# Stick-breaking attention by a running product: one sigmoid a score, the mask on another engine, the halves of the output added at the branch

## The chip, the core and the metric

The kernel runs on one core of one Trainium2 chip. The metric is the device time of one execution in microseconds (us). A measurement is the median of several executions; the profiles shown are one execution each. The core has five engines with an instruction queue each: PE (TensorE, matrix products), DVE (VectorE), ACT (ScalarE), POOL (GpSimd) and SP (SyncE, which here only issues DMAs). POOL issues DMAs too. An engine works through its queue in order: an instruction that waits holds up all that stand behind it.

## The reference

One decoder block on 1024 tokens of width 1024, all in float32. Three attention branches work on the normed input: stick-breaking attention (8 heads of 64), forgetting attention (8 heads of 64, called fox in the kernel) and attention over 256 memory tokens (4 heads of 128). Each branch has an output projection and a gate; the gated sum goes through `w_out`, then a squared-ReLU MLP follows. The part that the change touches:

```python
def stick_breaking_attention(q, k, v):
    # A[t,s] = beta[t,s] * prod_{s<j<t}(1-beta[t,j]), strictly causal
    ...
        z = einsum('bhtd,bhsd->bhts', q_block, k[:kend]) * scale
        strict = s_idx < t_idx
        log_rem = where(strict, log_sigmoid(-z), 0.0)
        after = cumsum(log_rem, axis=3, reverse=True) - log_rem
        w = where(strict, exp(log_sigmoid(z) + after), 0.0)
        out = einsum('bhts,bhsd->bhtd', w, v)
...
merged = gates[0] * (o_sb @ w_branch_sb) + gates[1] * (o_fox @ w_branch_fox) + gates[2] * (o_mem @ w_branch_mem)
x = x + merged @ w_out
```

With beta = sigmoid(z), what is left of the stick at token s is L[s], the product of sigmoid(-z) over the tokens from s to t; the weight of s is L[s+1] - L[s].

## The kernel before

**Split operands.** Every float32 operand of a product is kept as two tiles of 128 partitions, a rounded high part (`whi`, or the first half of an `h` tile) and the rest (`wlo`, or the second half). A product takes three matmuls: high by high, low by high, high by low. The high part is an ACT copy (L1054), the low part a DVE subtraction (L1055).

**Order of the work.** For about the first 925 us, each engine's order of instructions is set by a planner in the kernel: small programs (Python generators) yield `Op(engine, cost, ...)`, `Get(places)` for a free tile and events, and a machine model with the costs written in the kernel decides who goes next on each engine. The order is fixed before the run; at run time the engines only wait on semaphores. The output projection and the MLP behind it come in a fixed order of their own.

**Stick-breaking.** There are four pairs of heads. A unit is one head and 256 query rows (`g` of 4), that is two tiles of 128 rows; `UNITS` gives the order. `sb_tile` works through a tile's keys in chunks of up to 512 columns from the last to the first: PE makes the scores (L824) in a bank of PSUM; on the chunk with the diagonal DVE adds the mask, a tile `later` with a large number at the places not allowed (L834); ACT makes two sigmoids, `rho` = sigmoid(-z) in a scratch tile (L827, place from `RQ`) and sigmoid(z) (L828); DVE scans them backwards, state = rho * state + sigmoid(z) (L843), which is 1 - L. PE turns the result by 128x128 blocks (L917); ACT copies the turned bank as the high part `pth` (L922) and DVE makes the low part `ptl` (L924); PE multiplies with the split values (L934), whose rows were prepared as differences of neighbouring values by `value_step`.

**Output of a unit.** The product has 128 rows: the sums with the high and with the low half of the values, 64 rows each. For stick-breaking, ACT copies one half to `ob` (L962), DVE adds the other (L963), and one 64x256 store goes to `o_scr[0]` (L965). For fox, ACT copies all 128 rows (L953) and two stores put the halves in `o_scr[1]` and `low_scr` (L957, L958); `sums_kept` turns the softmax sums of a pair by PE (L614), ACT copies them (L616) and SP stores them in `l_scr` (L618).

**Branches.** `fetched_o(bi, k)` loads rows k of a branch's output as a 128x1024 tile from a place in `RR` (L1663); for fox (`bi` 2) it loads the low half too (L1666), adds it (L1668), and multiplies by the sums (L1672, L1675). `bring` then splits the tile as an operand. `dense_branch` runs the products (L1144) in the order memory, stick-breaking, fox (`bi` 0, 1, 2), multiplies by the gate (L1779, L1781, gates loaded at L1740) and adds (L1783). `RR` has three tiles of 128x1024; two of them serve as four `rho` tiles until the four stick-breaking pairs are over (`whole_again`), and `RR` then has all three again, with four `e` tiles more once all pairs are over.

**POOL** issues the loads of heads' keys and queries (L1004, L581) and of weights (L1062).

## Time and profile before

| what | value |
|---|---|
| device time, median of 3 runs | 1685.86 us (1685.47 to 1686.56) |
| profiled execution, first to last instruction | 1686.7 us |
| PE busy | 1675.3 us, 99% |
| DVE busy | 1293.0 us, 77% |
| ACT busy | 848.9 us, 50% |
| POOL busy | 255.2 us, 15% |
| DMA | 284.32 MB, mean 169 GB/s |

The profiled execution's span is 0.8 us above the median of the runs and 0.1 above their highest; no other time of that execution is shown. A line such as `L828 ACT ACTIVATE e<-pp 128x512 ... x31 | 17.3, 558 | 0.0` reads: line 828 of the kernel, engine, operation, output tile from input tile, shape, number of instructions, then busy time in us and mean of one in ns, then the engine's idle time just before them with what ended it. In a timeline a row begins with its start and its length in us; a bracket gives the idle time before it and what it waited for. A view of windows gives the busy time of each engine in a stretch, then the clock granted to PE (1.00 is full speed), the share of the DMA engines' time and the rate in GB/s.

### The profile page before, as it was taken

The page shows a single profiled execution, that of the slowest core. Times are in us where ns is not written, and L with a number is a line of the kernel's source. Part 1 is how long each engine was busy: PE and PEld are TensorE (multiplying, and loading weights), DVE is VectorE, ACT ScalarE, POOL GpSimd, SP SyncE. Part 2 cuts the span into 40 slices and gives each one's busy share as a digit, 9 for nine tenths or more (in the row PEclk, how much of TensorE's full clock was granted, in tenths as well). Part 3 has the DMA queues.
Part 4 walks back from the last instruction along what each step waited for, and adds up shares of the span by engine and source line. Part 5 has one row for each costly group of instructions (what it writes and reads, how often), then busy time and mean ns, then how long its engine had stood idle before and what let it go on. Part 6 is the DMA issues. An engine that isn't in the chain of part 4 may idle for free.

```text
span 1686.7 us, 25003 instructions
## 1 busy us (share of the span) xinstructions
PE 1675.3 (99%) x9118; PEld 1432.0 (85%) x9118; DVE 1293.0 (77%) x2079; ACT 848.9 (50%) x1474; POOL 255.2 (15%) x440
## 2 busy tenths in 40 slices
PE   9999999999999999999999999999999999999999
PEld 9998899998888888888888887878888887888887
DVE  7977778855459888867877898987777776688775
ACT  6455555534358888866761446433333344332331
POOL 0000000000253151254400011022111120000000
PEclk9999999999999999999999999999999999999999
DMA  7445434467475365387747542144444484564532
GB/s 245 157 150 182 149 119 150 146 194 243 127 232 161 111 186 151 117 240 224 236 146 245 183 162 100 57 162 155 152 150 137 150 307 171 202 202 143 198 125 75
DMA packets 142221, 284.32 MB, mean 169 GB/s; under 512 B 16913, under 2 KB 53329, under 8 KB 142098
## 3 DMA queue, kind: packets, MB, share of 16 engines
q1 hardware_dynamic: 110562, 183.08, 32.0%
q0 software_dynamic: 31536, 99.64, 19.5%
q8 instruction: 72, 1.18, 0.3%
q14 instruction: 51, 0.42, 0.1%
HBM read 189.83 MB, written 92.83 MB: 168 GB/s over the span
## 4 chain that ended last, share of the span: by engine, by line
PE 92%; DVE 5%; DMA 2%; ACT 1%; issue 1%; SPq 0%; DVEq 0%; ACTq 0%
PE pp L1456 11%; PE pp L1144 10%; PE pp L1981 10%; PE pp L2658 8%; PE sc L1456 7%; PE sc L1144 6%; PE sc L1981 5%; PE sc L2658 4%; PE tr L2658 4%; PE tr L917 4%; PE pv L1456 3%; PE pv L2658 3%; PE tr L1981 2%; PE sc L934 2%; PE pp L934 2%; DVE h L1917 1%
## 5 line engine op out<-in xcount | busy, mean ns | idle before, releaser
L1055 DVE TENSOR_TENSOR wlo<-raw,whi 128x1024 fp32r<-128x1024 f32 (+1 forms) x88 | 107.5, 1222 | 80.2 <-ACT whi L1054 80.0
L1054 ACT ACTIVATE whi<-raw 128x1024 fp32r<-128x1024 f32 (+1 forms) x88 | 93.2, 1059 | 78.8 <-PE pp L1456 32.7
L2658 PE MATMUL pp<-h,sop 128*128 128x512 f32 x540 | 128.4, 396 | 0.0
L2658 PEld LDWEIGHTS pp<-h,sop 128*128 128x128 f32 x540 | 101.6, 188 | 24.4
L1981 PE MATMUL pp<-h,oh 128*128 128x512 f32 x384 | 121.1, 397 | 0.7 <-ACT cu L2066 0.6
L924 DVE TENSOR_TENSOR ptl<-tr,pth 128x512 fp32r<-128x512 f32 (+1 forms) x160 | 99.1, 628 | 24.1 <-ACT pth L922 23.1
L922 ACT ACTIVATE pth<-tr 128x512 fp32r<-128x512 f32 (+1 forms) x160 | 87.4, 556 | 36.0 <-PE sc L934 15.8
L1981 PEld LDWEIGHTS pp<-h,oh 128*128 128x128 f32 x384 | 72.0, 188 | 19.0 <-ACT cu L2066 1.4
L2573 ACT ACTIVATE h<-t 128x2048 fp32r<-128x2048 f32 (+1 forms) x17 | 30.7, 1814 | 110.2 <-DVE t L1917 97.4
L1373 POOL DMA_DIRECT2D raw<-w_in x32 | 24.2, 755 | 395.1 <-DVE wlo L1055 395.1
L1144 PE MATMUL sc<-h,whi 128*128 128x512 f32 (+1 forms) x254 | 77.7, 389 | 0.0
L1456 PE MATMUL pp<-h,whi 128*128 128x512 f32 x248 | 77.5, 394 | 0.0
L1981 PE MATMUL pp<-h,ol 128*128 128x512 f32 x192 | 76.1, 396 | 0.0
L1456 PE MATMUL pp<-whi,h 128*128 128x256 f32 x384 | 71.8, 283 | 0.0
L843 DVE TENSOR_TENSOR_SCAN e<-r,e 128x384 f32<-128x384 f32 (+3 forms) x64 | 66.3, 1044 | 6.9 <-ACT e L828 6.5
L1974 ACT ACTIVATE oh<-raw 128x512 fp32r<-128x512 f32 x64 | 39.4, 625 | 61.8 <-DVE raw L1917 61.8
L2658 PE MATMUL sc<-h,sop 128*128 128x512 f32 x264 | 63.7, 396 | 0.0
L2658 PE MATMUL tr<-h,sop 128*128 128x512 f32 x264 | 63.4, 396 | 0.0
L1917 DVE TENSOR_TENSOR sop<-ur,sop 128x2048 fp32r<-128x2048 f32 (+1 forms) x28 | 61.8, 2211 | 2.0 <-ACT sop L2586 2.0
L917 PE MATMUL tr<-ident,e 128*128 128x128 f32 x416 | 62.7, 273 | 0.0
L1456 PEld LDWEIGHTS pp<-whi,h 128*128 128x128 f32 x384 | 60.2, 188 | 0.0
L2658 PEld LDWEIGHTS sc<-h,sop 128*128 128x128 f32 x264 | 49.6, 188 | 12.3 <-DVE sop L1917 0.5
(558 smaller groups left out, 5087.7 us busy)
## 6 DMA issues: line engine op xcount, KB each, us to landing
ur<-s_scr SPq DMA_DIRECT2D x26, 1024.0 KB
raw<-w_in POOLq DMA_DIRECT2D x42, 512.0 KB, 4.9
raw<-w_up SPq DMA_DIRECT2D x60, 256.0 KB
...
```

Of the source, the lines that this page charges most:

```text
L843: nc.vector.tensor_tensor_scan(out=back, data0=rho[:, :u][:, ::-1], data1=back, initial=0.0 if last else beta[:, c + u:c + u + 1], op0=ALU ...
L917: nc.tensor.transpose(tr[:, jj * 256 + a * P:jj * 256 + (a + 1) * P], es[a][:, j * P:(j + 1) * P], ident)
L922: yield Op("ACT", act_time(512 - lo_c), lambda: nc.scalar.activation(ph[:, lo_c:], tr[:, lo_c:], AF.Copy))
L924: yield Op("DVE", dve_time(512 - lo_c), lambda: nc.vector.tensor_tensor(pl[:, lo_c:], tr[:, lo_c:], f32(ph[:, lo_c:]), ALU.subtract))
L934: nc.tensor.matmul(pv[0][:, c_:256], pair.v[:, j, b, :], p_[:, jj * 256 + c_:(jj + 1) * 256], start=(k == 0 and n_ == 0 and i == 0), stop= ...
L1054: yield Op("ACT", 0.03 + act_time(m), lambda: nc.scalar.activation(hi, raw, AF.Copy))
L1055: yield Op("DVE", dve_time(m), lambda: nc.vector.tensor_tensor(lo, raw, f32(hi), ALU.subtract))
L1144: nc.tensor.matmul(ps, a_, b_, start=(first and i == 0), stop=(last and i == n - 1))
L1456: nc.tensor.matmul(out_, a_, b_, start=(first and n == 0 and j == 0), stop=(last and n == 3 and j == len(todo) - 1), skip_group_check=True)
L1917: nc.vector.tensor_tensor(out_, a_, b_, op)
L1981: nc.tensor.matmul(ps, w[a_][:, k * P:(k + 1) * P], h[b_][k], start=(first and k == 0 and i == 0), stop=(last and k == 3 and i == 2), skip ...
L2658: nc.tensor.matmul(ps, a_[:, c, qs], b_[:, c, :], start=(kind in ("P1", "P2", "P7") and c == 0 and i == 0), stop=(kind in ("P2", "P4", "P3 ...
```

## The change

- `sb_tile` makes one sigmoid a chunk, of the scaled score, straight into the tile `left` (L827); the other sigmoid goes, and with it the scratch tiles (`RQ`).
- The mask is no longer added to the scores by DVE. On the diagonal block, behind the sigmoid, POOL writes ones at the places that aren't allowed (an affine select of 128x128, L833).
- The scan is a product of what is left, in place, with a broadcast zero as the second operand and 1.0 at its start (L838).
- At the turned copy ACT adds minus one (a bias that is a pointer to a column of constants, L917) and DVE does the same with a number (L920), for stick-breaking only.
- The values' difference changes its sign (`value_step`).
- A stick-breaking unit's output is copied whole (L949) and stored as two halves, in `o_scr[0]` and `low_scr[0]` (L953, L954), as fox does. `fetched_o` for that branch takes two tiles of `RR`, loads both halves (L1645, L1648) and DVE adds them (L1649).
- All three tiles of `RR` are free from the start of the attention part, and `whole_again` goes.

Unchanged code stands up to eighteen lines earlier than before: turns at L911, the copies at L917 and L920, products of values at L931, sums of fox at L613 to L619, splits at L1044 and L1045, branch products at L1134, gates at L1727.

```diff
...
-    sm = C.p.tile([P, 8], F32, tag="sm", name="sm")
-    zero, one = sm[:, 0:1], sm[:, 1:2]
+    sm = C.p.tile([P, 9], F32, tag="sm", name="sm")
+    zero, one, minus = sm[:, 0:1], sm[:, 1:2], sm[:, 8:9]
...
+    nc.vector.memset(minus, -1.0)
...
-    low_scr = dram.tile([512, S], F32, name="low_scr", tag="low_scr")
+    low_scr = [dram.tile([512, S], F32, name=f"low_scr{b}", tag=f"low_scr{b}") for b in range(2)]
...
-    def sb_tile(pair, b, i, beta):
+    def sb_tile(pair, b, i, left):
...
         def chunk(ci, c, m, u):
-            rho = yield Get(RQ)
             sc = yield Get(SC)
+            part = left[:, c:c + u]
 
             def scores():
                 nc.tensor.matmul(sc[:, :m], q, pair.t["k1", b, ci][:, :m], start=True, stop=False)
                 nc.tensor.matmul(sc[:, :m], q, pair.t["k2", b, ci][:, :m], start=False, stop=True)
-
-            def sigmoids():
-                nc.scalar.activation(rho[:, :u], sc[:, :u], AF.Sigmoid, scale=HD ** -0.5)
-                nc.scalar.activation(beta[:, c:c + u], sc[:, :u], AF.Sigmoid, scale=-HD ** -0.5)
-
             yield Op("PE", 2 * mm_time(max(m, 256)), scores)
+            yield Op("ACT", act_time(u), lambda: nc.scalar.activation(
+                part, sc[:, :u], AF.Sigmoid, scale=HD ** -0.5), table=AF.Sigmoid)
+            SC.put(sc)
             last = c + u == n
             if last:
-                dg = sc[:, u - P:u]
-                yield Op("DVE", 0.22, lambda: nc.vector.tensor_tensor(
-                    dg, dg, holder["later"][:, 385:513], ALU.add))
-            yield Op("ACT", act_time(u, u), sigmoids, table=AF.Sigmoid)
-            SC.put(sc)
-            if not last:
+                dg = left[:, n - P:n]
+                yield Op("POOL", 0.3, lambda: nc.gpsimd.affine_select(
+                    out=dg, in_=dg, pattern=[[-1, P]], compare_op=ALU.is_ge, fill=1.0, base=-1, channel_multiplier=1))
+            else:
                 yield scanned
-
-            def scan():
-                back = beta[:, c:c + u][:, ::-1]
-                nc.vector.tensor_tensor_scan(out=back, data0=rho[:, :u][:, ::-1], data1=back,
-                                             initial=0.0 if last else beta[:, c + u:c + u + 1],
-                                             op0=ALU.mult, op1=ALU.add)
-            yield Op("DVE", 0.1 + 0.00215 * u, scan, 0.14)
-            RQ.put(rho)
+            back = part[:, ::-1]
+            yield Op("DVE", 0.1 + 0.00215 * u, lambda: nc.vector.tensor_tensor_scan(
+                out=back, data0=back, data1=zero.to_broadcast([P, u]),
+                initial=1.0 if last else left[:, c + u:c + u + 1], op0=ALU.mult, op1=ALU.add), 0.14)
             if last:
                 machine.fire(scanned)
 
...
-        scr, r0 = o_scr[0 if pair.kind == "sb" else 1], (2 * pair.p + b) * HD
+        of_sb = pair.kind == "sb"
+        scr, low, r0 = o_scr[0 if of_sb else 1], low_scr[0 if of_sb else 1], (2 * pair.p + b) * HD
...
             ph = yield Get(PH)
-            yield Op("ACT", act_time(512 - lo_c), lambda: nc.scalar.activation(ph[:, lo_c:], tr[:, lo_c:], AF.Copy))
+            h_, t_ = ph[:, lo_c:], tr[:, lo_c:]
+            yield Op("ACT", act_time(512 - lo_c), lambda: nc.scalar.activation(
+                h_, t_, AF.Identity, bias=minus) if of_sb else nc.scalar.activation(h_, t_, AF.Copy))
             pl = yield Get(PL)
-            yield Op("DVE", dve_time(512 - lo_c), lambda: nc.vector.tensor_tensor(
-                pl[:, lo_c:], tr[:, lo_c:], f32(ph[:, lo_c:]), ALU.subtract))
+            yield Op("DVE", dve_time(512 - lo_c), lambda: nc.vector.scalar_tensor_tensor(
+                pl[:, lo_c:], t_, -1.0, f32(h_), ALU.add, ALU.subtract) if of_sb else nc.vector.tensor_tensor(
+                pl[:, lo_c:], t_, f32(h_), ALU.subtract))
...
         ob = yield Get(OB)
         rows, cols = slice(r0, r0 + HD), slice(g * 256, (g + 1) * 256)
-        if pair.kind == "fox":
-            yield Op("ACT", act_time(256), lambda: nc.scalar.activation(ob, pv[0][:, :256], AF.Copy))
-            PV.put(pv[0])
-
-            def halves():
-                nc.sync.dma_start(scr[rows, cols], ob[:HD, :])
-                nc.sync.dma_start(low_scr[rows, cols], ob[HD:, :])
-            yield Op("SP", 0.2, halves, 3.0)
-        else:
-            o = ob[:HD, :]
-            yield Op("ACT", act_time(256), lambda: nc.scalar.activation(o, pv[0][HD:P, :256], AF.Copy))
-            yield Op("DVE", dve_time(256), lambda: nc.vector.tensor_tensor(o, o, pv[0][0:HD, :256], ALU.add))
-            PV.put(pv[0])
-            yield Op("SP", 0.1, lambda: nc.sync.dma_start(scr[rows, cols], o), 2.5)
+        yield Op("ACT", act_time(256), lambda: nc.scalar.activation(ob, pv[0][:, :256], AF.Copy))
+        PV.put(pv[0])
+
+        def halves():
+            nc.sync.dma_start(scr[rows, cols], ob[:HD, :])
+            nc.sync.dma_start(low[rows, cols], ob[HD:, :])
+        yield Op("SP", 0.2, halves, 3.0)
...
     def value_step(c, g, a, b, more):
         yield Sleep(3.0)
-        yield Op("DVE", dve_time(512), lambda: nc.vector.tensor_tensor(a, a, b, ALU.subtract))
+        yield Op("DVE", dve_time(512), lambda: nc.vector.tensor_tensor(a, b, a, ALU.subtract))
...
         opened("A", (HT, "h", 12, 512, F32R), (VV, "v", 2, 2048, F32R), (EL, "e", 4, D, F32), (RR, "r", 3, D, F32),
-               (LATER, "later", 1, 513, F32))
+               (LATER, "later", 1, 512, F32))
         later = holder["later"] = LATER.free[0]
-        halves = [RR.free.popleft() for _ in range(2)]
-        RQ.put(*(t[:, i * 512:(i + 1) * 512] for t in halves for i in range(2)))
-        spawn(whole_again(halves))
...
-    def whole_again(tiles_):
-        for pair in pairs[:4]:
-            yield pair.over
-        RR.put(*tiles_)
-
...
     def fetched_o(bi, k):
 
-        raw_ = yield Get(RR)
+        raw_, *low_ = (yield Get(RR, 2)) if bi == 1 else [(yield Get(RR))]
         raw, rows = raw_[:, :S], slice(k * P, (k + 1) * P)
         yield from transfer(lambda: nc.sync.dma_start(raw, o_scr[order[bi][1]][rows, :]), P * S * 4)
+        if bi == 1:
+            t = low_[0]
+            yield from transfer(lambda: nc.sync.dma_start(t, low_scr[0][rows, :]), P * S * 4)
+            yield Op("DVE", dve_time(S), lambda: nc.vector.tensor_tensor(raw, raw, t, ALU.add))
+            RR.put(t)
         if bi == 2:
             t = yield Get(RR)
-            yield from transfer(lambda: nc.sync.dma_start(t, low_scr[rows, :]), P * S * 4)
+            yield from transfer(lambda: nc.sync.dma_start(t, low_scr[1][rows, :]), P * S * 4)
             yield Sleep(1.0 if k == ks[3] else 2.0)
             yield Op("DVE", dve_time(S), lambda: nc.vector.tensor_tensor(raw, raw, t, ALU.add))
```

The planner orders its part anew. PE's order is the same up to about 485 us of the trace before, and from about 922 us on.

**SP where the memory branch ends and the stick-breaking branch begins.** Before (near 881 us of the trace), L1663 loads `r_4694` and `r_4696` for fox, L1666 the low half for fox; the four loads of the stick-breaking branch stand further ahead and aren't in these rows:

```order
L957 DMA o_scr_75<-ob_4803 64x256
L958 DMA low_scr<-ob_4803 64x256
L1663 DMA r_4694<-o_scr_75 128x1024
L1740 DMA o_4811<-gate_scr 128x512
L618 DMA l_scr<-ob_4805 16x128
L1740 DMA o_4810<-gate_scr 128x512
L1666 DMA r_4695<-low_scr 128x1024
L1663 DMA r_4696<-o_scr_75 128x1024
```

After, with `o_scr_75` and `low_scr_78` the halves of stick-breaking, `o_scr_76` and `low_scr_79` those of fox:

```order
L1648 DMA r_4697<-low_scr_78 128x1024
L953 DMA o_scr_76<-ob_4804 64x256
L954 DMA low_scr_79<-ob_4804 64x256
L1727 DMA o_4812<-gate_scr 128x512
L1727 DMA o_4813<-gate_scr 128x512
L619 DMA l_scr<-ob_4806 16x128
L1645 DMA r_4697<-o_scr_75 128x1024
L1645 DMA r_4696<-o_scr_76 128x1024
L1645 DMA e_4692<-o_scr_76 128x1024
L1648 DMA r_4698<-low_scr_78 128x1024
L1653 DMA e_4693<-low_scr_79 128x1024
L1653 DMA e_4694<-low_scr_79 128x1024
```

The last operand of the stick-breaking branch is now loaded in two halves behind the store of the fox sums, with two fox loads between them and two behind.

**PE at the same place.** Before (`whi_163`, `wlo_164` and `h_7212` are split outputs of stick-breaking, `whi_167` and `wlo_168` weights):

```order
L1144 MATMUL sc_136<-whi_163,whi_167 128x512
L1144 MATMUL sc_136<-wlo_164,whi_167 128x512
L1144 MATMUL sc_136<-whi_163,wlo_168 128x512
L1144 MATMUL sc_136<-h_7212,whi_167 128x512 x2
L1144 MATMUL sc_136<-h_7212,wlo_168 128x512
L1144 MATMUL pp_134<-whi_163,whi_167 128x512
L1144 MATMUL pp_134<-wlo_164,whi_167 128x512
L1144 MATMUL pp_134<-whi_163,wlo_168 128x512
L614 MATMUL tr_139<-ident,fn 16x128
```

After (`whi_165`, `wlo_166` and `h_7517` are split outputs of stick-breaking, the other `h` tiles earlier ones, `whi_169` and `wlo_170` weights):

```order
L1134 MATMUL pp_136<-h_4681,whi_169 128x512
L1134 MATMUL pp_136<-h_4687,whi_169 128x512
L1134 MATMUL pp_136<-h_4681,wlo_170 128x512
L615 MATMUL tr_140<-ident,fn 16x128
L1134 MATMUL sc_138<-whi_165,whi_169 128x512
L1134 MATMUL sc_138<-wlo_166,whi_169 128x512
L1134 MATMUL sc_138<-whi_165,wlo_170 128x512
L1134 MATMUL sc_138<-h_7517,whi_169 128x512 x2
L1134 MATMUL sc_138<-h_7517,wlo_170 128x512
```

The turn of the fox sums, which stood behind the first products of the last two stick-breaking operands, now stands three products ahead of the first that needs `h_7517`.

**DVE at the same place, after.** `r_4696` and `r_4697` are stick-breaking outputs that are summed at L1649:

```order
L1649 TENSOR_TENSOR r_4696<-r_4696,r_4697 128x1024
L613 RECIPROCAL fn<-fn 128x16
L1045 TENSOR_TENSOR h_7518<-r_4698,h_7518 128x512
L1045 TENSOR_TENSOR wlo_166<-r_4696,whi_165 128x512
L1045 TENSOR_TENSOR h_7518<-r_4698,h_7518 128x512
L1045 TENSOR_TENSOR wlo_166<-r_4696,whi_165 128x512
L1045 TENSOR_TENSOR wlo_168<-raw_171,whi_167 128x1024
L1649 TENSOR_TENSOR r_4697<-r_4697,r_4698 128x1024
L1045 TENSOR_TENSOR h_7517<-r_4697,h_7517 128x512 x2
```

The reciprocal that the turn of the fox sums needs stands behind the first sum, and the split of `h_7517` behind the second; before there were no sums here.

**SP at the memory branch's loads.** Before (near 727 us):

```order
L965 DMA o_scr_74<-ob_4805 64x256
L703 DMA o_scr_76<-o_4811 128x512
L1641 DMA gate_scr<-o_4810 128x512
L1663 DMA r_4696<-o_scr_76 128x1024
L1663 DMA r_4694<-o_scr_76 128x1024
L1663 DMA r_4695<-o_scr_76 128x1024
```

After, where the memory attention ends later in the order:

```order
L704 DMA o_scr_77<-o_4812 128x512
L619 DMA l_scr<-ob_4806 16x128
L1645 DMA r_4698<-o_scr_77 128x1024
L1645 DMA r_4696<-o_scr_77 128x1024
L1645 DMA r_4697<-o_scr_77 128x1024
```

The three loads now stand behind a store of fox sums.

**POOL in the stick-breaking part, after.** Selects stand between loads of heads' keys and queries; before, this queue had loads only:

```order
L833 AFFINE_SELECT es_4809<-es_4809 128x128
L833 AFFINE_SELECT es_4810<-es_4810 128x128
L582 DMA h_4820<-mq_scr_92 128x512
L582 DMA h_4818<-mq_scr_93 128x512
L994 DMA h_4685<-sbk_scr_86 64x512 x2
L994 DMA h_4814<-sbk_scr_87 64x512 x2
L994 DMA h_4683<-sbk_scr_86 64x512 x2
L994 DMA h_4817<-sbk_scr_87 64x512 x2
L994 DMA h_4819<-sbq_scr_84 64x512
L994 DMA h_4819<-sbq_scr_85 64x512
```

The next select (`es_4807`) follows these loads.

4 lines of the change are left out of this document (2 added, 2 removed).

## The prediction

> **What bounds the kernel now.** I read the page's busy times, then the waits of PE, then windows and timelines of the planned part. The first is a line of the page, the second the two longest waits of PE (engine, line waited for: total, times, longest), the third two stretches of 100 us.
>
> ```profile
> PE 1675.3 (99%) x9118; PEld 1432.0 (85%) x9118; DVE 1293.0 (77%) x2079; ACT 848.9 (50%) x1474; POOL 255.2 (15%) x440
> ```
> ```profile
> PE pp L2305 <- ACT h L2280: 1.5, 1, 1.5
> PE pv L869 <- DVE st L874: 1.5, 1, 1.5
> ```
> ```profile
> 600.00:700.00 100.00, 100.00 (x625) 88.19 (x624) 87.82 (x162) 89.39 (x197) 32.88 (x60) 1.00 0.55 163
> 700.00:800.00 100.00, 98.53 (x609) 86.03 (x608) 73.77 (x202) 70.21 (x158) 45.66 (x85) 0.98 0.72 213
> ```
>
> PE is the bound: 1675.3 of 1686.7 us, and in the stick-breaking stretch (600 to 700) it is full although ACT and DVE also stand near 88%. An instruction taken from ACT or DVE there gives nothing by itself. Only one stall lies in the part that the change touches: 1.5 us at L869, at 742.59. The timelines of SP, ACT and PE, and windows around it (PE, PEld, DVE, ACT, POOL busy, granted clock, DMA share, GB/s):
>
> ```profile
> 731.58 0.33 SPq L1663 DMA_DIRECT2D r<-o_scr  x1
> ```
> ```profile
> 740.50 0.63 ACT L1054 ACTIVATE h<-r 128x512 fp32r<-128x512 f32 x1 [3.58 <-DMA r<-o_scr]
> ```
> ```profile
> 742.59 0.50 PE L869 MATMUL pv<-h,h 128*128 128x512 f32 x1 [1.47 <-DVE st L874]
> ```
> ```profile
> 742.00:744.00 2.00, 1.41 (x6) 1.05 (x7) 2.00 (x7) 1.72 (x4) 0.00 (x0) 0.94 0.98 340
> 744.00:746.00 2.00, 2.00 (x6) 1.52 (x6) 0.81 (x5) 1.91 (x4) 0.00 (x0) 0.50 0.98 320
> 746.00:748.00 2.00, 2.00 (x13) 1.70 (x12) 0.70 (x2) 0.46 (x2) 0.00 (x0) 0.71 0.81 308
> ```
>
> A 512 KB load issued at 731.58 landed at 740.5, 8.9 us later, with the DMA near full; ACT stood behind it for 3.58 us, and what PE waited for stood behind ACT. The granted clock then fell: 2 x 0.06 + 2 x 0.50 + 2 x 0.29 = 1.7 us lost. So this one late load costs 1.5 + 1.7 = 3.2 us, and that is the most that the planned part can give back.
>
> **The change, part by part.** Durations of the work that goes or comes, by groups:
>
> ```profile
> L828 ACT ACTIVATE e<-pp 128x512 f32<-128x512 f32 (+3 forms) x31 | 17.3, 558 | 0.0
> L828 ACT ACTIVATE e<-pv 128x512 f32<-128x512 f32 (+3 forms) x33 | 16.7, 507 | 0.0
> L828 ACT ACTIVATE es<-pp 128x256 f32<-128x256 f32 (+3 forms) x16 | 7.6, 472 | 0.0
> L828 ACT ACTIVATE es<-pv 128x128 f32<-128x128 f32 (+3 forms) x16 | 6.8, 425 | 0.0
> L738 ACT ACTIVATE sn<-tr,sm 128x512 fp32r<-128x512 f32 x26 | 17.5, 684 | 10.8 <-PE tr L732 10.4
> L922 ACT ACTIVATE pth<-tr 128x512 fp32r<-128x512 f32 x96 | 57.2, 599 | 14.2 <-PE sc L934 11.0 <-PE pp L934 2.4 <-PE tr L917 0.5
> ```
> ```profile
> L834 DVE TENSOR_TENSOR pv<-pv,later 128x128 f32<-128x128 f32 x38 | 10.9, 287 | 3.9 <-PE pv L824 3.7
> L843 DVE TENSOR_TENSOR_SCAN e<-r,e 128x512 f32<-128x512 f32 x40 | 50.4, 1264 | 3.5 <-ACT e L828 3.1
> L1323 DVE TENSOR_TENSOR_SCAN sn<-sn,sm 8x512 f32<-8x512 f32 x2 | 2.4, 1208 | 0.0
> L963 DVE TENSOR_TENSOR ob<-ob,sc 64x256 f32<-64x256 f32 x18 | 7.2, 400 | 2.0 <-ACT ob L962 1.9
> L1668 DVE TENSOR_TENSOR r<-r,r 128x1024 f32<-128x1024 f32 x3 | 3.7, 1217 | 0.0
> ```
> ```profile
> L1563 POOL TENSOR_SCALAR_AFFINE_SELECT later<-later 128x129 f32<-128x129 f32 x1 | 0.3, 293 | 0.1
> L1004 POOL DMA_DIRECT2D h<-fxk_scr x48 | 25.3, 535 | 78.1 <-PE pv L870 33.7 <-PE pp L870 23.3 <-PE pv L824 18.8
> ```
>
> Sigmoid: ACT loses the second one, 17.3 + 16.7 + 7.6 + 6.8 = 48.4 us. Mask: DVE loses 64 x 0.287 = 18.4 us, POOL gains 64 x 0.293 = 18.8 us. Scan: the zero that is broadcast in place of a second tile should cost nothing: a scan of that form took 1208 ns on 8 rows of 512, one with two full tiles 1264 on 128 rows; bounds 0 to 0.06 us gained each. Turned copy: 80 stick-breaking blocks take a pointer, so 684 in place of 599 ns, at most 80 x 0.085 = 6.8 us more of ACT; the DVE instruction with a number as an operand replaces one of the same size, and I take no difference, since nothing waits on a few tens of ns. Output: DVE loses 32 x 0.400 = 12.8 us and gains four adds of 1.217 us, 4.9 us; ACT's eviction keeps its length; SP gains 32 stores of 64 KB and four loads of 512 KB.
>
> All of this lies beside PE. The chain that PE waits for is sigmoid (0.56), select (0.29), two scans of at most 1.26: 3.4 us. By the two orders, counted in PE's work at 0.23 us for a product of 512 columns, the shortest distance from a tile's last score to the turn that reads its scan grows from 3.7 to 6.8 us, the median from 8.6 to 15.8. The cover exists and the terms are 0; if it were gone, each tile would show its select, 18.8 us in all (a rival below).
>
> One thing speaks against the select. DVE and POOL did lengthen each other once: of eight POOL products at L2251 one took 3081 ns and the others some 1.3 us, while at the same place a DVE pair took 2.92 us and not 1.29.
>
> ```profile
> L2251 POOL TENSOR_TENSOR h<-h,gb x8: 1301/1315/3081, 988.7 to 1042.8; 128x512 f32<-128x512 f32 x8
> ```
> ```profile
> 991.11 2.92 DVE L1917 TENSOR_TENSOR h<-raw,h 128x512 f32<-128x512 f32 x2
> ```
>
> By that row a select may stand behind one scan: 3.4 + 1.26 = 4.7 us, still under 6.8. The Trainium skill, page "SBUF — State Buffer", section "SBUF: two separate sides", says that DVE and GpSimd share a port pair which one instruction holds to its end while the other fully blocks; the two rows agree, and the rule would put each select behind whatever scan or split runs, with the rival's sum if the cover is shorter than I count.
>
> The 742 stall. The three loads of the memory branch's operands now stand behind a store of fox sums and a transpose of PE, with most of the next pair's key loads already through. Gain 3.2 if the stall goes, 0 if another takes its place; I take 2.5, since the crowd is smaller.
>
> The junction between the first and the second branch is the term that decides. Today PE runs through it (its rows; then ACT's, SP's and DVE's):
>
> ```profile
> 880.80 0.39 PE L1144 MATMUL sc<-whi,whi 128*128 128x512 f32 x1
> 881.49 0.62 PE L1144 MATMUL sc<-h,whi 128*128 128x512 f32 x2
> 882.87 0.27 PE L614 MATMUL tr<-ident,fn 128*16 128x128 f32 x1
> ```
> ```profile
> 883.18 0.27 ACT L616 ACTIVATE ob<-tr 16x128 f32<-16x128 f32 x1 [1.97 <-PE tr L614]
> ```
> ```profile
> 881.08 0.33 SPq L1663 DMA_DIRECT2D r<-o_scr  x1
> 883.47 0.32 SPq L618 DMA_DIRECT2D l_scr<-ob  x1
> 883.88 0.38 SPq L1740 DMA_DIRECT2D o<-gate_scr  x1
> 884.31 0.42 SPq L1666 DMA_DIRECT2D r<-low_scr  x1
> ```
> ```profile
> L1054 ACT ACTIVATE h<-r 128x512 fp32r<-128x512 f32 x16 | 9.8, 627 | 5.9 <-DMA r<-o_scr 5.9
> ```
> ```profile
> L1055 DVE TENSOR_TENSOR h<-r,h 128x512 fp32r<-128x512 f32 x16 | 10.7, 685 | 3.4 <-ACT h L1054 3.3
> ```
> ```profile
> raw<-w_in POOLq DMA_DIRECT2D x42, 512.0 KB, 4.9
> raw<-w_b POOLq DMA_DIRECT2D x9, 512.0 KB, 5.5
> ```
> ```profile
> 885.00:895.00 10.00, 10.00 (x45) 8.13 (x44) 6.74 (x10) 1.06 (x1) 0.75 (x1) 1.00 0.99 336
> ```
>
> Before, every stick-breaking operand is split ahead of the transpose of the fox sums (L614), and the store of those sums (L618) holds up only fox loads. In the new order the last stick-breaking operand (`h_7517`) is needed three products after the transpose: 881.49 - 880.80 = 0.69 us, with the transpose 0.72. Its two loads stand on SP behind that store (now L619), which waits for ACT, which waits for PE's transpose. Counted from the transpose: ACT at +0.31, the store at +0.60, the next load at +1.0 (883.88 - 882.87). Three more loads follow; the next to it reuses a tile whose second half has to be split first, at about +1.7 (ACT 0.63, DVE 0.69, partly overlapped), and at 0.4 us an issue the low half leaves at about +2.5. A 512 KB load lands after 4.9 us (median of 42), or 8.9 as at 731.58: +7.4 to +11.4. Four of them, 2.1 MB at 336 GB/s, are 6.2 us from +1.0, so no earlier by bytes either. Then the add, 1.22, the first split, 0.63, and some 0.2 us for the low half behind it: ready at +9.4 to +13.4. Less 0.72, PE stands 8.7 to 12.7 us. I take 11, above the middle, because seven loads go out together and this place already ran at a DMA share of 0.99.
>
> The sum ahead of it (`r_4696`) waits for a low half loaded some 7.8 us of PE work before: 0.4 to issue, 5.5, 1.22 and 0.63 is 7.8, so 0; with 8.9 it is 3.3. I take 1. The clock after the long idle time: 1.7 us as after 742, bounds 0 and 3.4 (twice). The dip is not certain after each wait, as the other 1.5 us stall shows, its window at full clock:
>
> ```profile
> 1024.00:1026.00 2.00, 0.84 (x8) 0.84 (x9) 1.93 (x5) 1.93 (x5) 0.00 (x0) 1.00 0.93 245
> ```
>
> The Trainium skill, page "TensorE: Matmul & The Clock Gate", section "Part 1: The HAM clock gate", has the clock halve after at least one idle window of about 3.4 us, with windows that run free. Here 1.5 us at 742 sufficed and 1.5 us at 1025 did not, so the measurement decides against that length; by the rule a wait of 11 us would surely trip it, and the sum would keep its 1.7.
>
> Sum against the profiled execution: 1686.7 - 2.5 + 11 + 1 + 1.7 = 1697.9. That execution is 0.8 above the median of the three runs (1685.86), so 1697.
>
> **The rivals.** (a) Other side: the junction isn't felt and the 742 stall goes with its dip: 1685.86 - 3.2 = 1682.7, and 1682 with a few waits under 0.25 us. It needs the low half to leave SP some 9 us sooner than its place in the queue allows. For it: the transpose could be reached late, after waits that ACT and SP don't share; against it: load and product hang on the same transpose, so the distance stays. (b) The junction costs little, because a quick landing and a gain elsewhere cancel: within 0.2%, 1683 to 1689. It would take a landing in about 3 us, below every row. (c) The loads crowd: if the low half lands with all seven loads, 3.7 MB at 336 GB/s is 10.9 us; with 2.7 us on top (8.9 less the 6.2 above) it is there at +14.6, the stall 15.9, the clock lost twice: 1686.7 - 2.5 + 15.9 + 1 + 3.4 - 0.8 = 1704. (d) POOL becomes the bound: selects stand behind scans, or behind a block of a dozen key loads in POOL's queue (12 x 0.535 = 6.4 us, which with 3.4 exceeds the shortest cover of 6.8). If each of the 64 selects shows, 1685.86 + 18.8 = 1704.7. Against it: the blocks are few, the median cover 15.8.
>
> **How the numbers follow.** 0.2% is 3.4 us, about what a measurement of this kernel can tell from no change. The forecast (1691 to 1702) has 0.73, (c) 0.11, (d) 0.04, (b) 0.07, (a) 0.05. Faster is (a), the same (b), slower the others, 0.88. Bounds added up one way: -3.2 + 8.7 = +5.5, 1691; the other way 12.7 + 3.3 + 3.4 = +19.4, 1705; all ends at once being unlikely, the range is 1690 to 1704.
>
> **What would show it.** Right: a wait of PE of 8 to 13 us at the dense products (now L1134) for the split of `h`, near 882, with ACT waiting for DVE's sum and that for `r<-low_scr`; a granted clock of 0.5 behind it; no wait at L869's successor near 742; PE still full from 500 to 700, ACT there some 10 to 15 points emptier. Wrong: no wait of PE above 2 us near 882, or waits at the turns of stick-breaking tiles for scans, with selects well above 0.3 us.

## The result, and the profile after

The changed kernel took 1711.18 us (median of 4 executions, 1709.69 to 1712.98), the kernel before 1686.16 beside it (1685.47 to 1686.56): a ratio of 1.015, interval 1.0135 to 1.0164. That is 25 us slower. The direction was forecast; the size was not (1697, range to 1704). The page, and the longest waits of PE, of the changed kernel:

```profile
span 1711.1 us, 25019 instructions
...
PE 1684.5 (98%) x9118; PEld 1436.1 (84%) x9118; DVE 1274.8 (75%) x1988; ACT 808.9 (47%) x1370; POOL 286.3 (17%) x504
```
```profile
PE sc L1134 <- ACT h L1044: 10.0, 1, 10.0
PE tr L911 <- DVE ptl L920: 3.8, 1, 3.8
PE pp L2292 <- ACT h L2267: 1.9, 1, 1.9
...
PE tr L911 <- DVE ptl L921: 1.1, 1, 1.1
```

ACT and DVE do less, as planned, and PE waits more. The first row is the stall that was forecast. The second was not forecast. The third was 1.5 us before. The wait at L869 is gone. In windows of 100 us (PE, PEld, DVE, ACT, POOL busy, granted clock, DMA share, GB/s) the loss stands in two places. Before:

```profile
500.00:600.00 100.00, 100.00 (x628) 88.53 (x627) 88.13 (x154) 84.36 (x190) 25.94 (x47) 1.00 0.46 140
...
800.00:900.00 100.00, 100.00 (x618) 87.64 (x617) 79.88 (x188) 61.41 (x141) 22.05 (x39) 1.00 0.67 205
```

After:

```profile
500.00:600.00 100.00, 94.72 (x585) 83.41 (x584) 72.76 (x101) 61.95 (x125) 46.35 (x87) 0.97 0.56 161
...
800.00:900.00 100.00, 89.92 (x561) 77.88 (x559) 72.56 (x172) 57.76 (x132) 21.32 (x38) 0.97 0.66 200
```

PE runs the same number of matmuls in both kernels (9118), so the loss can be placed. At the last matmul before the two orders part (484.7 us before, 485.9 after, by the tiles' names) the changed kernel is 1.2 us late, at the first one from which they agree again (922.6 and 945.2) 22.6, at PE's last 24.7. For the planned part I took each PE instruction's distance to the next, less the distance that its shape takes when nothing waits (0.232 us for 512 columns), and summed that excess by stretch:

| stretch, us | before | after | difference |
|---|---|---|---|
| 475 to 500 | 1.3 | 0.6 | -0.7 |
| 500 to 600, the first stick-breaking units | 10.5 | 19.3 | +8.8 |
| 600 to 725 | 13.0 | 14.5 | +1.5 |
| 725 to 775, the memory branch's loads | 9.0 | 5.6 | -3.4 |
| 775 to 850 | 10.1 | 9.7 | -0.3 |
| 850 to 925, the junction | 3.7 | 19.3 | +15.6 |

The differences sum to 21.5, and the delay grows by 21.4, from 1.2 to 22.6.

**The junction went as forecast.** PE, ACT, SP and DVE of the changed kernel:

```profile
889.57 0.27 PE L615 MATMUL tr<-ident,fn 128*16 128x128 f32 x1
...
901.26 1.52 PE L1134 MATMUL sc<-h,whi 128*128 128x512 f32 x2 [9.95 <-ACT h L1044]
```
```profile
890.22 0.25 ACT L617 ACTIVATE ob<-tr 16x128 f32<-16x128 f32 x1
...
900.58 1.15 ACT L1044 ACTIVATE h<-r 128x512 fp32r<-128x512 f32 x2 [8.64 <-DVE r L1649]
```
```profile
890.49 0.32 SPq L619 DMA_DIRECT2D l_scr<-ob  x1
890.91 1.15 SPq L1645 DMA_DIRECT2D r<-o_scr  x2
892.17 0.37 SPq L1645 DMA_DIRECT2D e<-o_scr  x1
892.59 0.42 SPq L1648 DMA_DIRECT2D r<-low_scr  x1
```
```profile
899.32 1.23 DVE L1649 TENSOR_TENSOR r<-r,r 128x1024 f32<-128x1024 f32 x1 [6.12 <-DMA r<-low_scr]
```

From the transpose the low half leaves at +3.0 (forecast +2.5), lands after 6.7 us (4.9 to 8.9), and PE resumes at +11.7 (+9.4 to +13.4). The clock after it:

```profile
902.00:904.00 2.00, 2.00 (x6) 1.61 (x6) 2.00 (x3) 0.00 (x0) 0.00 (x0) 0.50 0.30 114
904.00:906.00 2.00, 2.00 (x7) 1.52 (x6) 2.00 (x4) 0.00 (x0) 0.00 (x0) 0.50 0.46 135
906.00:908.00 2.00, 2.00 (x8) 1.64 (x7) 1.30 (x3) 0.00 (x0) 0.00 (x0) 0.72 0.99 236
```

With the 0.74 us of work before 902 at half clock, 0.37 + 1 + 1 + 0.56 = 2.9 us are lost there. The 1.1 us wait near 856 is DVE standing behind the first of the four sums, which waited 1.77 us for its low half and held up a low part of fox (`ptl`, L921). The sum to which the prediction gave 1 us, the one ahead of the last, cost PE a wait of 0.2 us.

**What was missed: the first units.** POOL, DVE and PE of the changed kernel from 509 us:

```profile
509.05 3.64 POOL L994 DMA_DIRECT2D h<-sbk_scr  x7
516.40 0.53 POOL L994 DMA_DIRECT2D h<-sbk_scr  x1 [3.71 <-DMA v<-v_sb]
517.82 2.06 POOL L994 DMA_DIRECT2D h<-sbq_scr  x4 [0.89 <-DMA h<-sbk_scr]
519.88 0.79 POOL L833 TENSOR_SCALAR_AFFINE_SELECT e<-e 128x128 f32<-128x128 f32 x3
520.62 3.97 POOL L833 TENSOR_SCALAR_AFFINE_SELECT es<-es 128x128 f32<-128x128 f32 x4
```
```profile
520.22 4.92 DVE L838 TENSOR_TENSOR_SCAN e<-e,sm 128x512 f32<-128x512 f32 x5 [4.38 <-POOL e L833]
525.06 1.12 DVE L920 SCALAR_TENSOR_TENSOR ptl<-tr,pth 128x384 fp32r<-128x384 f32 x2
```
```profile
521.51 0.39 PE L1134 MATMUL pp<-g,wlo 128*128 128x512 f32 x1
525.74 0.66 PE L911 MATMUL tr<-ident,e 128*128 128x128 f32 x2 [3.83 <-DVE ptl L920]
```

POOL had twelve key and query loads to issue before the next select, and twice waited with them for the DMA (3.71 and 0.89 us). DVE stood idle 4.38 us for a select, then had five scans in a row ahead of the low part (`ptl`) that PE needed. The clock fell behind this stall too:

```profile
526.00:528.00 2.00, 2.00 (x12) 2.00 (x10) 2.00 (x4) 0.58 (x1) 2.00 (x4) 0.50 0.90 197
528.00:530.00 2.00, 2.00 (x9) 1.81 (x8) 2.00 (x3) 0.88 (x2) 1.07 (x3) 0.50 1.02 272
530.00:532.00 2.00, 2.00 (x6) 1.54 (x6) 2.00 (x4) 1.06 (x2) 1.74 (x4) 0.59 1.04 284
```

Here 1 + 1 + 0.82 = 2.8 us; with stalls of 0.9 us at 508.8, 3.8, and 0.5 near 566 that is 8.0 of the 8.8. The one near 566 has the same form: a select behind another block of loads, then three scans ahead of the low part. The one at 508.8 came the other way round. A load of weights (L1052) stood in POOL's queue behind four selects and left at 498.4; the sigmoid that PE waited for stood on ACT behind the split of that load:

```profile
506.14 1.06 ACT L1044 ACTIVATE whi<-raw 128x1024 fp32r<-128x1024 f32 x1 [1.63 <-DMA raw<-w_in]
```

In mask_dve (below), where no select stands in that queue, the same load left at 488.6, and ACT did not wait for it.

### The profile page after: what moved, and what is told of

Its sections match the earlier page's. It is cut to its first block, busy times and chain, and to the rows that moved or that the text cites. A ratio compares the mean times of both kernels' runs of the same rounds, so it can differ in the third digit from the quotient of the medians.

```text
span 1711.1 us, 25019 instructions
## 1 busy us (share of the span) xinstructions
PE 1684.5 (98%) x9118; PEld 1436.1 (84%) x9118; DVE 1274.8 (75%) x1988; ACT 808.9 (47%) x1370; POOL 286.3 (17%) x504
## 3 DMA queue, kind: packets, MB, share of 16 engines
q0 software_dynamic: 31536, 99.64, 19.2%
## 4 chain that ended last, share of the span: by engine, by line
PE 84%; DVE 5%; DMA 2%; issue 2%; POOL 1%; ACT 1%; SPq 0%; POOLq 0%; ACTq 0%; DVEq 0%
PE pp L1968 10%; PE pp L1446 10%; PE pp L1134 8%; PE pp L2645 8%; PE sc L1446 7%; PE sc L1968 5%; PE sc L1134 5%; PE sc L2645 4%; PE tr L2645 4%; PE tr L911 3%; PE pv L1446 3%; PE pv L2645 3%; PE tr L1968 2%; PE pp L931 2%; PE sc L931 2%
## 5 line engine op out<-in xcount | busy, mean ns | idle before, releaser
L1045 DVE TENSOR_TENSOR wlo<-raw,whi 128x1024 fp32r<-128x1024 f32 (+1 forms) x88 | 107.6, 1223 | 90.2 <-ACT whi L1044 89.8
L1044 ACT ACTIVATE whi<-raw 128x1024 fp32r<-128x1024 f32 (+1 forms) x88 | 93.1, 1058 | 88.5 <-PE pp L1446 32.8
L1134 PE MATMUL sc<-h,whi 128*128 128x512 f32 (+1 forms) x248 | 77.0, 393 | 10.0 <-ACT h L1044 10.0
L838 DVE TENSOR_TENSOR_SCAN e<-e,sm 128x512 f32<-128x512 f32 (+3 forms) x64 | 66.0, 1052 | 12.5 <-POOL e L833 11.8
L911 PE MATMUL tr<-ident,e 128*128 128x128 f32 x416 | 63.1, 276 | 5.0 <-DVE ptl L920 3.8
L917 ACT ACTIVATE pth<-tr,sm 128x384 fp32r<-128x384 f32 (+1 forms) x80 | 51.0, 645 | 32.9 <-PE pp L931 12.8
L920 DVE SCALAR_TENSOR_TENSOR ptl<-tr,pth 128x384 fp32r<-128x384 f32 (+1 forms) x80 | 49.4, 626 | 22.8 <-ACT pth L917 22.5
L911 PEld LDWEIGHTS tr<-ident,e 128*128 128x128 f32 x416 | 50.2, 142 | 15.5 <-issue 4.2
L921 DVE TENSOR_TENSOR ptl<-tr,pth 128x512 fp32r<-128x512 f32 (+1 forms) x80 | 50.3, 633 | 16.9 <-ACT pth L918 16.5
```

The lines of the kernel that those rows point to most:

```text
L838: yield Op("DVE", 0.1 + 0.00215 * u, lambda: nc.vector.tensor_tensor_scan(out=back, data0=back, data1=zero.to_broadcast([P, u]), initial=1 ...
L911: nc.tensor.transpose(tr[:, jj * 256 + a * P:jj * 256 + (a + 1) * P], es[a][:, j * P:(j + 1) * P], ident)
L917: yield Op("ACT", act_time(512 - lo_c), lambda: nc.scalar.activation(h_, t_, AF.Identity, bias=minus) if of_sb else nc.scalar.activation(h ...
L921: pl[:, lo_c:], t_, -1.0, f32(h_), ALU.add, ALU.subtract) if of_sb else nc.vector.tensor_tensor(
L1044: yield Op("ACT", 0.03 + act_time(m), lambda: nc.scalar.activation(hi, raw, AF.Copy))
L1045: yield Op("DVE", dve_time(m), lambda: nc.vector.tensor_tensor(lo, raw, f32(hi), ALU.subtract))
```

## The experiments

Two theories stood at the start. Theory Q with J: two late arrivals cost the 25 us, the selects behind POOL's loads and the low half at the junction. Against it: the new order itself, or the new instructions, cost it wherever they are placed. The table gives each kernel's median, its ratio to the kernel before as run beside it (medians of 1685.56 to 1686.78), and the excess of PE in three stretches of its profile, as above. The medians are of 4 executions, those of no_low and store_act of 2, those of old_order and old_order_copy of 11. The excess is that of one execution: in the changed kernel, mask_dve and keys_sp, which have the same order there, 850 to 950 lay between 19.2 and 20.6.

| kernel | us | ratio, interval | 500 to 600 | 700 to 850 | 850 to 950 |
|---|---|---|---|---|---|
| before | 1686.16 | | 10.5 | 21.8 | 3.7 |
| after | 1711.18 | 1.015 (1.0135 to 1.0164) | 19.3 | 18.4 | 19.3 |
| mask_dve | 1705.69 | 1.011 (1.0093 to 1.0127) | 11.8 | 18.9 | 20.6 |
| keys_sp | 1707.93 | 1.0126 (1.0111 to 1.0141) | 12.0 | 19.4 | 19.2 |
| old_out | 1708.68 | 1.013 (1.0115 to 1.0145) | 14.6 | 31.8 | 4.8 |
| both_loads | 1702.69 | 1.0094 (1.0079 to 1.011) | 15.1 | 18.8 | 12.5 |
| no_low | 1700.43 | 1.0086 (1.0067 to 1.0104) | 14.7 | 18.2 | 10.3 |
| store_act | 1708.05 | 1.0131 (1.0112 to 1.0149) | 13.9 | 18.9 | 18.0 |
| both_mask | 1699.85 | 1.0081 (1.0068 to 1.0095) | 11.8 | 18.1 | 12.4 |
| fetch_first | 1696.99 | 1.0064 (1.0049 to 1.0079) | 11.8 | 18.2 | 10.6 |
| scan_only | 1693.54 | 1.0045 (1.003 to 1.006) | 10.6 | 23.0 | 3.5 |
| out_only | 1704.14 | 1.0107 (1.009 to 1.0124) | 10.8 | 19.6 | 20.1 |
| old_order | 1689.64 | 1.0021 (1.0012 to 1.003) | 10.7 | 21.8 | 3.8 |
| old_order_copy | 1688.21 | 1.001 (1.0001 to 1.0019) | 10.7 | 19.3 | 3.3 |

### mask_dve: the mask off POOL, the order kept

```diff
-                yield Op("POOL", 0.3, lambda: nc.gpsimd.affine_select(
-                    out=dg, in_=dg, pattern=[[-1, P]], compare_op=ALU.is_ge, fill=1.0, base=-1, channel_multiplier=1))
+                yield Op("POOL", 0.3, lambda: nc.vector.scalar_tensor_tensor(
+                    dg, holder["later"][:, 385:513], 1.0, dg, ALU.min, ALU.max))
...
```

The rest of the edit makes the mask tile `later` one column wider and shifts its diagonal. The planner still counts the instruction as POOL's, so the order stays.

> The changed kernel with its order of work kept; only the ones on the diagonal block are written by DVE (maximum with a mask tile, about 0.29 us) in place of POOL's select, at the same point of the order. Theory Q (the selects came late because they stand on POOL behind loads of heads' keys that wait for the DMA): the stall of 3.8 us at 525.7, the two small ones near it and the halved clock behind them go, 500 to 575 loses 6 to 8.5 us, and the time is 1702 to 1705. Theory P (the plan brings the first tiles too late whichever engine masks): the stall stays, the time is 1709 to 1713. The junction's stall of 10 us near 891 stays by both.

1705.69. At the point where the changed kernel stood 3.8 us, PE now goes straight on, as its timeline shows (the same two instructions as above):

```profile
519.90 0.39 PE L1134 MATMUL pp<-g,wlo 128*128 128x512 f32 x1
520.14 0.55 PE L911 MATMUL tr<-ident,e 128*128 128x128 f32 x3
```

500 to 600 fell by 7.5 us, as Theory Q has it; theory P is out. By the medians the gain is 5.5 us. The total is 0.7 over the forecast; in the profiled execution the junction's wait was longer than in the changed kernel's (its row of PE's waits):

```profile
PE sc L1134 <- ACT h L1044: 13.0, 1, 13.0
```

### keys_sp: the loads off POOL, the selects left there

```diff
-                        nc.gpsimd.dma_start(f32(t[k][rows_, :]), src)
+                        (nc.gpsimd if fox else nc.sync).dma_start(f32(t[k][rows_, :]), src)
...
```

The values' load for stick-breaking is issued by SP in the same way.

> The changed kernel with its order of work kept; only the loads of keys, queries and values of the stick-breaking heads are issued by SP in place of POOL, so that no such load stands ahead of a select. Selects stay on POOL, beside DVE's scans. Theory Q (loads ahead in POOL's queue): the stall at 525.7 goes, 1702 to 1706. Theory L (selects and scans hold each other up: selects took up to 1.25 us beside scans and 0.29 alone): the stall stays, 1708 to 1713. Side risk: SP's stores now wait behind loads, so small waits of ACT for an output tile may show.

1707.93, over the 1702 to 1706 of Theory Q and just under the range of L. The trace decides between them: no wait of 3.8 us is left, and 500 to 600 is back to 12.0. The side cost came a little earlier, where PE now waits for a load (475 to 500 rose from 0.6 to 2.8), and the junction's wait was 12.3:

```profile
PE sc L1135 <- ACT h L1045: 12.3, 1, 12.3
PE pp L824 <- DMA h<-sbq_scr: 1.9, 1, 1.9
```

So the loads ahead of the selects made the stall. Selects are held up beside scans, as the durations of the changed kernel's selects say (minimum, median, maximum in ns), but that alone did not show on PE:

```profile
L833 POOL TENSOR_SCALAR_AFFINE_SELECT e<-e x32: 282/292/1172, 485.7 to 677.1; 128x128 f32<-128x128 f32 x32
L833 POOL TENSOR_SCALAR_AFFINE_SELECT es<-es x32: 287/444/1251, 492.6 to 680.8; 128x128 f32<-128x128 f32 x32
```

### old_out: the output part undone

Put into the changed kernel, from the kernel before (and the load and sum of the low half leave `fetched_o`):

```diff
-        yield Op("ACT", act_time(256), lambda: nc.scalar.activation(ob, pv[0][:, :256], AF.Copy))
...
+            o = ob[:HD, :]
+            yield Op("ACT", act_time(256), lambda: nc.scalar.activation(o, pv[0][HD:P, :256], AF.Copy))
+            yield Op("DVE", dve_time(256), lambda: nc.vector.tensor_tensor(o, o, pv[0][0:HD, :256], ALU.add))
+            PV.put(pv[0])
+            yield Op("SP", 0.1, lambda: nc.sync.dma_start(scr[rows, cols], o), 2.5)
...
```

> The changed kernel with its output part undone: DVE adds the two halves of a stick-breaking unit's output at its eviction and one half is stored, as before the change; the planner orders anew. Theory J (the junction's stall comes from the low halves loaded late behind the store of fox sums): no wait over 2 us near 891, 850 to 925 back within 2 us of the kernel before, 1695 to 1698, with the stall near 525 still there. Rival (the branch would wait for other loads there, since all go out late): a wait of 4 us or more stays near 891, over 1702. If the 742 stall of the kernel before comes back, add 3 to either.

1708.68: over the range of J, and over 1702 as the rival has it, but not for the rival's reason. The junction is as J expects (4.8 against 3.7, no wait over 2 us). The new order has a loss of its own near the memory branch, 31.8 from 700 to 850 against 18.4. PE's wait there, then ACT and SP:

```profile
PE tr L911 <- DVE ptl L921: 5.5, 3, 3.9
```
```profile
772.64 0.63 ACT L1051 ACTIVATE whi<-r 128x512 fp32r<-128x512 f32 x1 [2.78 <-DMA r<-o_scr]
```
```profile
766.05 0.32 SPq L619 DMA_DIRECT2D l_scr<-ob  x1
766.47 2.59 SPq L1652 DMA_DIRECT2D r<-o_scr  x3
```

Three loads of 512 KB go out at 766.5, the first is used by ACT at 772.6, and what PE waits for stands behind ACT, as at 742 in the kernel before. The kernel's late load has moved.

### both_loads: the two halves loaded back to back

```diff
+        def loads():
+            nc.sync.dma_start(raw, o_scr[order[bi][1]][rows, :])
+            if bi == 1:
+                nc.sync.dma_start(low_[0], low_scr[0][rows, :])
+        yield from transfer(loads, (2 if bi == 1 else 1) * P * S * 4, 0.2 if bi == 1 else 0.1)
-        yield from transfer(lambda: nc.sync.dma_start(raw, o_scr[order[bi][1]][rows, :]), P * S * 4)
...
-            yield from transfer(lambda: nc.sync.dma_start(t, low_scr[0][rows, :]), P * S * 4)
```

> The changed kernel with both halves of a stick-breaking output issued back to back (before, the low half left only when the planner took the high half as landed); the planner orders anew. Theory J1 (position of the low half in SP's queue sets the end of the stall): it leaves about 1.3 us sooner and has two fox loads fewer ahead of it, the stall near 891 falls from 10 to 5 to 8 us, 1705 to 1709. Rival J2 (bytes of the whole crowd set the landing): the stall stays within 1 us of 10, 1710 to 1712.

1702.69, below what either theory gave: the wait fell to 6.5 us, as J1 has it, and the new order also lost less from 500 to 600 (15.1).

```profile
PE sc L1134 <- ACT h L1044: 6.5, 1, 6.5
```

### no_low: the low halves left out, the order kept

```diff
-            yield from transfer(lambda: nc.sync.dma_start(t, low_scr[0][rows, :]), P * S * 4)
-            yield Op("DVE", dve_time(S), lambda: nc.vector.tensor_tensor(raw, raw, t, ALU.add))
+            yield from transfer(lambda: None, P * S * 4)
+            yield Op("DVE", dve_time(S), lambda: None)
```

> The changed kernel with its order kept; the low halves of the stick-breaking output are neither loaded nor added (this part of the sum is left out). The last operand then waits only for its high half, which still stands behind the store of fox sums and left SP at 890.9. Theory J: the stall near 891 falls from 10 to 3 to 6 us (landing 5 to 6 us after the issue, 0.63 for the split, less the 0.7 of products), 1703 to 1706. Rival (the operand waits for something else than these loads): the stall stays above 8, 1709 to 1713.

1700.43, and the wait is 4.5 us, in the range of J:

```profile
PE sc L1134 <- ACT h L1044: 4.5, 1, 4.5
```

So a bit more than half of the stall is the low half, its landing and its add; the rest is the high half that itself goes out late. (With no low half loaded at all, the high half also travels in a smaller crowd, so the split between the two is rough.) The total is lower than forecast; 500 to 600 cost less in this execution (14.7 against 19.3 with the same order), so the select stall there varies between executions.

### store_act: the store of fox sums off SP, the order kept

```diff
-        yield Op("SP", 0.1, lambda: nc.sync.dma_start(
+        yield Op("SP", 0.1, lambda: nc.scalar.dma_start(
             l_scr[h0:h0 + 2, :].rearrange("h (i p) -> (h i) p", p=P), t[:16, :P]), 2.5)
```

> The changed kernel with its order kept; the stores of fox sums (L619) are issued by ACT, so that no load on SP stands behind them. Theory S (the store holds up the last stick-breaking operand's loads, as the prediction has it): high half 1.7 us sooner, the low half up to 1.7 us sooner, stall 8 to 9, about 1709. Rival T (the low half is held by the fox load ahead of it, which waits for a tile until the second half of wlo is made, 0.9 us ahead of the low half's issue): the low half leaves at the same time, the stall stays within 0.7 us of 10, 1710 to 1712. Landing times of four loads spread by some 3 us between runs, so the issue times decide, not the total.

1708.05. The wait of PE did not shrink, it was 11.5. SP's rows, to be read against a transpose at 883.8:

```profile
883.21 2.92 SPq L1645 DMA_DIRECT2D r<-o_scr  x2
886.29 0.32 SPq L1645 DMA_DIRECT2D e<-o_scr  x1
886.66 0.42 SPq L1648 DMA_DIRECT2D r<-low_scr  x1
```

The high half leaves 0.6 us ahead of the transpose, no longer 1.3 behind it, but the low half leaves at +2.9 in place of +3.0. By the times of issue, which the expectation lets decide, that is rival T: the store was not what held the low half. The fox load ahead of it was (the second of the two loads in the first row): it left at 885.8, when DVE had ended the split that reads its tile:

```profile
885.10 0.69 DVE L1045 TENSOR_TENSOR wlo<-r,whi 128x512 fp32r<-128x512 f32 x1
```

The low half landed after 8.3 us here, 6.7 in the changed kernel, and so the wait of 11.5 lies outside T's range, as the total does.

### both_mask and fetch_first: the remedies together

both_mask is both_loads with the mask of mask_dve; fetch_first is both_mask with one rule more (`sb_here` is a list of events, one for each operand):

```diff
...
             RR.put(t)
+            machine.fire(sb_here[k])
...
     def last_operands(in_O):
+        for ev in sb_here:
+            yield ev
         for i, place in enumerate((0, 2, 3, 1)):
...
```

> Both remedies at once in the order of both_loads: the two halves of a stick-breaking output are loaded back to back, and DVE writes the ones on the diagonal in the place of POOL's select. If the two costs are separate, 1702.7 less the 3.5 us that both_loads still has over mask_dve from 500 to 575 gives 1699 (1697 to 1701), with a stall of 6 to 9 us left at the junction. If the late selects' cost only moves, it stays at 1702 or more.

1699.85, the forecast to 1 us: the two costs are separate, and 12.4 us of excess stay from 850 on, with a wait of 7.1 us at the junction.

> both_mask with one rule more for the planner: no fox operand is fetched until all four stick-breaking operands are summed, so that the fox branch can't take the tiles that the last stick-breaking operand needs; the last low half then stands on SP ahead of the store of fox sums. Theory J (the stall at the junction is this one late operand): no wait over 2 us there, 875 to 925 falls by 8 to 10 us, 1690 to 1692. Rival M (the lateness moves on to the fox operands): a wait of 3 us or more at the start of the fox branch, some 25 us later, 1694 or more.

1696.99. The junction's excess is gone (850 to 925 gives 2.2), but the wait reappears at the start of the fox branch, 4.0 us at 931.6, with the clock behind it: 8.4 us from 925 to 950. That is rival M. Row of PE's waits:

```profile
PE sc L150 <- ACT h L1044: 4.0, 1, 4.0
```

### scan_only and out_only: each half of the change alone, ordered anew

scan_only is old_out with the mask as in mask_dve, planned for DVE; out_only is the kernel before with the change's lines in `unit` and `fetched_o`, the reverse of old_out's diff:

```diff
...
-                yield Op("POOL", 0.3, lambda: nc.gpsimd.affine_select(
...
+                yield Op("DVE", 0.22, lambda: nc.vector.scalar_tensor_tensor(
...
```

> Of the change only the arithmetic and the freed tiles: one sigmoid, product scan, minus one at the turned copy; DVE writes the ones on the diagonal, with its cost known to the planner; the output's halves are added at the eviction as before. The planner orders anew. If all that was lost comes from the select on POOL and from the low halves, it is at most 2 us from the kernel before, 1684 to 1688. If each new order brings a late load of its own (as old_out had one of 12 us at the memory branch), 1690 or more, with that wait seen between 700 and 900.

1693.54. No stall at either place; what it loses over the kernel before stands partly at 750 to 775 (6.8 against 3.4), in several waits under 0.8 us. The arithmetic with a new order is slower by 7 to 8 us, not the 0 to 2 that the first half of the expectation gave. The time is that of the second half, 1690 or more, but no single late load shows: most of the loss isn't placed.

> The kernel before with the output part alone: stick-breaking outputs stored as two halves and added at the branch; two sigmoids, mask by DVE on the scores, and the old scratch tiles stay. The planner orders anew. Theory J: the low halves of the last operand come late here too, a wait of 5 to 13 us at the first products of the stick-breaking branch, none near 510 to 530, 1691 to 1700. Rival (the junction's stall needs the new order of the stick-breaking part): no wait over 2 us there, 1684 to 1688.

1704.14, above the range. The junction is there without any other part of the change, and worse: two waits, for two operands in turn.

```profile
PE sc L1138 <- ACT whi L1048: 7.9, 1, 7.9
PE sc L1138 <- ACT h L1048: 4.7, 1, 4.7
```

So the output part alone, in an order of its own, makes the junction's stall; it doesn't need the new stick-breaking part. That it is worse here may come from the scratch tiles, which stay and leave `RR` smaller; no run shows that.

### old_order and old_order_copy: the new arithmetic in the old order

```diff
-                nc.scalar.activation(rho[:, :u], sc[:, :u], AF.Sigmoid, scale=HD ** -0.5)
-                nc.scalar.activation(beta[:, c:c + u], sc[:, :u], AF.Sigmoid, scale=-HD ** -0.5)
+                nc.scalar.activation(beta[:, c:c + u], sc[:, :u], AF.Sigmoid, scale=HD ** -0.5)
...
-                nc.vector.tensor_tensor_scan(out=back, data0=rho[:, :u][:, ::-1], data1=back,
-                                             initial=0.0 if last else beta[:, c + u:c + u + 1],
+                nc.vector.tensor_tensor_scan(out=back, data0=back, data1=zero.to_broadcast([P, u]),
+                                             initial=1.0 if last else beta[:, c + u:c + u + 1],
```

with the turned copy and `value_step` of the change in old_order. old_order_copy keeps the plain turned copy: it leaves out the minus one, and is there for its time alone.

> The kernel before with its order of work and its output kept; only the arithmetic of the change is put in: one sigmoid a chunk (behind the old mask on the scores by DVE), the scan as a running product, minus one at the turned copy. ACT does some 41 us less (48.4 us of second sigmoids less 6.8 us of pointers). Theory O (PE bounds, what was lost came from the order and the loads): no stall near 525 or 881, the 742 stall stays, time 1684 to 1687, that is the same as before. Rival W (the saved ACT work was worth something): 1680 to 1683. Rival C (the new instructions themselves cost): above 1689.

1689.64, 1.0021 of the kernel before, or 4 us: over theory O's range, and just above the 1689 of rival C. So the new instructions do cost something in the old order too. Taking a sigmoid from each chunk gave nothing. There is no wait in the planned part above 0.7 us; in this profile the 1.5 us wait near 742 is not there either, against theory O, though the order is that of the kernel before.

> old_order with the turned copy as before the change: a plain copy and a plain difference; minus one is not added there (that part of the arithmetic is left out). old_order came 4 us above the kernel before, 1689.6, with no wait of PE above 0.7 us in the planned part. Theory I (the pointer of the turned copy, 0.09 us on each of 80 copies in the chain turn, copy, difference, product, costs what old_order lost): 1685 to 1687. Rival S (one sigmoid less shifts when ACT is free, and the loss has nothing to do with the copies): 1689 to 1690. If between, both.

1688.21, 1.001: between theory I and rival S. By the ratios the copies carry about half of what old_order lost (0.11 of 0.21%), though the two intervals overlap. Where the other half comes from isn't settled: no single wait holds it. All of old_order's loss is at most 0.3%, 5 us of the changed kernel's 25.

Put together by the medians: without the late selects the changed kernel is 5.5 us faster (mask_dve), without the low halves 10.8 (no_low), and fetch_first, with both remedies, 14.2. Of the 11 us that fetch_first still loses, the wait that moved on to the fox branch and the clock behind it are the largest part that is placed; the new arithmetic (some 4 us in the old order) and the new order itself hold the rest, and how they share it is not shown.

No version here beats the kernel before; the best that holds a part of the change is old_order, and the measurement puts it 0.1 to 0.3% behind.

## Why the prediction was right and wrong, point by point

- **PE bounds, so work saved on ACT and DVE is worth nothing.** Right. ACT's busy time fell by 40 us and DVE's by 18, and old_order shows no gain. It even lost 0.12 to 0.30%, where the new instructions were put at nothing. PE was full from 600 to 700, as foretold, with ACT at 77% in place of 89%, but not from 500 to 600 (94.72%).
- **"All of this lies beside PE ... the terms are 0."** This step failed, and it cost the forecast most: 8.8 us from 500 to 600 in the profile, 5.5 by the medians of the changed kernel and mask_dve. The cover was counted on PE's side (6.8 us between a score and its turn) against a chain of sigmoid, select and scans. What POOL's queue puts ahead of a select was left to rival (d), at 0.04, because blocks of loads are few and their issue takes 6.4 us. But POOL also waits between such loads, 3.71 and 0.89 us here, and one late block made the 3.8 us stall and 2.8 us of slow clock behind it. mask_dve and keys_sp, which take away the selects or the loads, both remove it. Rival (d) had the mechanism and a wrong price: not 64 selects of 0.29 but one block. What it did not have is the way back, a load of weights late behind selects (0.9 us).
- **The junction.** Right in place, chain and size of the stall: 10.0 us against 11. The prediction names two gates for the low half, the store of fox sums and the fox load that waits for its tile (+1.7, measured +2.2); store_act shows that the second alone sets its time, and that the store held up only the high half. The clock cost 2.9 in place of 1.7. The 1 us for a sum came true by luck: the sum that it was meant for cost 0.2, and another, near 856, cost 1.1. Together 15.6 over the kernel before, against 13.7; 1.4 of the 15.6 is in none of these terms.
- **The 742 stall.** It went, as forecast, and 725 to 775 lost 3.4 us less than before. But that gain wasn't there to be had against the median. The profiled execution of before took 1686.7 us from first to last instruction at a mean clock of 0.999; seven later executions of the same kernel took 1683.4 to 1685.8 (median 1684.1), six of them at a mean clock of 1.000, which leaves no room for a dip like that behind 742. Of all 44 later ones, 40 were at 1.000, and neither old_order nor old_order_copy, in the same order, has a wait of PE over 0.7 us there. Counted from such an execution the sum is 1684.1 + 11 + 1 + 1.7 = 1697.8, and with the 1.7 us that a measured time has over its span (1685.84 less 1684.1) 1699.5: the base made the forecast 2.5 us too low.
- **The rest**, 1.5 us from 600 to 725 and some 2 us in the fixed part, is spread over differences below 1 us and was not in the sum.

Adding up, one profile against the other: 1711.1 less 1697.9 is 13.2 us. The first units give 8.8, the junction 1.9, the rest 1.5 and some 2, and 725 to 775 took off 0.9 more than the 2.5 of the forecast: 13.3. The profiled execution of the changed kernel is the longest of its four, 1.8 above the median, and its 8.8 is that execution's; with the same order and the select on POOL the stretch cost 3.4 and 4.2 us over before in store_act and no_low. Between the medians, 1711.2 and 1697, the miss is 14.2; 2.5 of the base and the 8.8, 1.9, 1.5 and 2, less 1.8, are 14.9. The account closes to about 1 us, not better.
